# Second mixture: four weight buffers used for two groups, and the recurrence's tables begun a group later at four steps a group

## The chip, the cores and the metric

The kernel runs on one core of a Trainium2 chip. The metric is the device time of one execution in microseconds (us). A core has five engines with a queue of instructions each: PE (TensorE, matmuls), DVE (VectorE), ACT (ScalarE), POOL (GpSimd) and SP (SyncE, which here does little but issue loads). Sixteen DMA engines move data between the chip's DRAM and the core's SBUF; here transfers are issued by SP and, for a few small things, by ACT. An engine takes its instructions in order, and an instruction waits on semaphores for what it needs.

## What is computed

The program is two blocks in a row. The first has two layers, each a mixer (attention) and a mixture of experts; the second is a dilated attention and a recurrence (a diagonal state space model). The mixture, cut to what matters here:

```python
def hier_moe(xt, wg, bg, we, be, w1, w3, w2):
    ...                       # two experts of 32 and a weight for each token
    def expert_block(args):
        xb, e = args
        hb = jax.nn.silu(xb @ w1[e]) * (xb @ w3[e])
        return hb @ w2[e]
    ...                       # weighted, and added to the tokens
```

An expert has w1 and w3 of 1024 x 512 and w2 of 512 x 1024, 6 MB in float32. The recurrence of the last block:

```python
    A = lax.complex(a_re.astype(f), a_im.astype(f))
    dt = jnp.exp(log_dt.astype(f))[:, None]
    a_bar = jnp.exp(A * dt)
    Bm = lax.complex(b_re.astype(f), b_im.astype(f))
    b_bar = ((a_bar - 1.0) / A)[..., None] * Bm
    ...
    _, states = lax.associative_scan(combine, (a_elems, bu), axis=1)
    y = jnp.einsum('bsgp,gcp->bsgc', states, Cm).real
```

Powers of a_bar, b_bar and products of both with C depend on parameters alone. The kernel makes tables of them long before the recurrence, beside the second mixture.

## The kernel before

**The mixture's groups.** The second layer's mixture (`moe(1)`) has 256 tokens and works through all 32 experts in ten groups, p0 to p9 (`groups`, L1330): p0 and p1 take two experts each with 64 token slots, p2 to p5 three experts with 64, 32 and 32 slots, p6 to p9 four with 32. Each group's weights are loads of 1 MB, six for each expert: 12 loads in p0 and in p1, 18 in p2 to p5, 24 in p6 to p9, 192 in all. `weights` (L1134) issues them on SP in the order h0 w1, h0 w3, h1 w1, h1 w3 (h is the half of the 1024 rows), then w2. "Load 13 of p5" counts them from 0 within a group; loads 1 to 24 without a group are those of p0 and p1 counted from 1.

**One group on PE.** `hidden` (L1258) has four blocks of matmuls L1264, called h0m0, h0m1, h1m0, h1m1 (m 0 is w1, m 1 is w3); each uses one load of each expert. Between their matmuls `scatter` puts the result of the group before back to its tokens (L1314, L1315 on PE, products yt L1317 on DVE, sums L1321 on POOL); with two blocks of tokens that is four pieces, all in h0m0 and h0m1. Then the next group's tokens are gathered (L1225, L1251), and `result` (L1290) multiplies by w2 (L1296); ACT and DVE take it out of PSUM as yh and yl (L1303, L1304). The one-hot matrix of the next group is made on DVE ahead of hidden's scatter.

**The weight buffers.** `slot` (L136) gives a load its buffer. From this mixture's start the ring has 11 (7 named wt, 4 named wu), used in turn, so that a load waits for PE to be done with the load eleven ring loads before it. Beside it `early_slots` opens a pool of four buffers of the same size (named we) on the other side of SBUF; it lives until `rest` (L1076) closes it. Before, only loads 9 to 12 of p0, its h1 parts of w1 and w3, come there. The ring's loads are freed by PE's hidden and result. SP issues in program order, so a load that waits holds up all behind it.

**The tables.** `rest()` is called once, in p1: it closes the early pool, opens another at its place (`xl`), loads the final gain (fg) and starts the generator `side = self.ssm_side(...)` (L1797). Each `next(side)` emits one step of the tables in place, on whatever engines it needs. `hidden` calls it after h0m0 and h0m1 (condition `h == 0`), and `groups` calls it once more behind the result: three steps a group from p1 on. The 24 steps, as far as they matter:

- step 1: five small loads on ACT's queue (L1816, L1820) and four loads of 256 KB on SP through the ring, called raw 0 to 3 (the matrices of B and C)
- step 2: two transposes (L1844) and an exponential on DVE
- step 3: PE transposes raw 0 and 1 (L1836); step 5 those of raw 2 and 3
- steps 4 and 6: small DVE work; step 7 is empty; step 8: powers of a_bar on DVE (L1923 to L1969)
- step 9: b_bar (L1989 to L2001); step 10: Bg of the first half (L2012, L2014, with POOL)
- step 11: 16 transposes of Bg (L2021), copied to cx, then a write of 1 MB to DRAM on ACT's queue, Sd<-cx (L2024)
- step 12: Wd on DVE (L2031, L2032); step 13: KC (matmuls L2037, DVE L2040, L2042), then a write of 128 KB, Sm<-KC (L2044)
- steps 14 to 17: the same as 10 to 13 for the second half; steps 18 to 24: small writes of CP, E and U (L2053), powers on DVE and POOL, at the end two writes of 1 MB

A step of a group stands in the program where it is called, and that sets the order on every engine: the whole stage is under `manual_schedule`, which keeps the written order.

**The completion counters.** Transfers issued by SP and ACT take eight counters in turn (DMAHW0 to 7 in the rows below). A transfer waits for the one before it on its counter, whichever queue issued that. So a weight load can wait for a table write that ACT has not yet issued.

Of the kernel before, what the change touches and what calls it, by code (L numbers as in the profile page):

```python
# [27 lines left out]
NRING = 7  # L28
NMORE = 4
NBMAX = 16  # L30
FIRST = 1
EARLY = (1, 4)
SOON = 3
AFF = "aaaa"
# [83 lines left out]
class Model:  # L118
# [17 lines left out]
    def slot(self):  # L136

        self.load += 1
        if self.early is not None and self.load > self.early[1]:
            pool, _, n = self.early  # L140
            if self.load - self.early[1] == n:
                self.early = None
            return pool.tile([P, 2048], F32, name="we", tag="w")
        if self.cycle:
            self.turn += 1
            return self.cycle[(self.turn - 1) % len(self.cycle)].tile([P, 2048], F32, name="wu", tag="w")
        if self.apart:
            return self.ring2.tile([P, 2048], F32, name="wu", tag="w")
        self.turn += 1
        n = NRING + self.nmore  # L150
        if self.ring2 is not None and (self.turn * self.nmore % n < self.nmore if self.mixed else
                                       (self.turn - 1) % n >= NRING):
            return self.ring2.tile([P, 2048], F32, name="wu", tag="w")
        return self.ring.tile([P, 2048], F32, name="wt", tag="w")
# [4 lines left out]
        self.turn = self.load = 0  # L159
        ctx.callback(self.fewer_slots)  # L160

    def early_slots(self, ctx, name, n):

        self.early = ctx.enter_context(self.tc.tile_pool(name=name, bufs=n, side="right")), 12 - n, n

    def fewer_slots(self):
        self.ring2 = self.cycle = None
# [855 lines left out]
    def moe(self, l):  # L1023
        nc, A, tc, m = self.nc, self.A, self.tc, self.m
        nb, nv, ctx, c2, pool, sb, pr = m.nb, m.nb // 2, m.ctx, m.c2, m.pool, m.sb, m.pr
# [42 lines left out]
        side, G2 = iter(()), None if l == 0 else m.G2  # L1068
# [27 lines left out]
        def slots(ts):  # L1096

            at = [32 * sum(ts[:j]) for j in range(len(ts) + 1)]
            rs = [slice(a, b) for a, b in zip(at, at[1:])]
            w = 64 if ts == PAIR else 32  # L1100
            return rs, [(j, slice(a, a + w)) for j, r in enumerate(rs) for a in range(r.start, r.stop, w)]
# [116 lines left out]
        def gather(OH, rv, ts, pxs=None):  # L1218

            xg = xe.tile([P, D], F32, name="xg")  # L1220
            for n in range(2):
                px = pxs[n] if pxs else m.pp.tile([P, 512], F32, name=f"px{n}")
                for i in range(nb if pxs is None else 0):
                    for src in (hh, hl):
                        nc.tensor.matmul(px, lhsT=OH[:, i, :], rhs=src[:, i, 4 * n:4 * n + 4, :],  # L1225
                                         start=(i == 0 and src is hh), stop=(i == nb - 1 and src is hl))
                if n == 0:
                    nc.scalar.activation(xg[:, 0:512], px, AF.Copy)
                else:
                    nc.vector.tensor_copy(xg[:, 512:], px)  # L1230
            pid = psum.tile([P, 512], F32, name="tr", bufs=2)
            for i in range(nb):
                nc.tensor.matmul(pid[:, 0:4 * len(ts)], lhsT=OH[:, i, :], rhs=rv[:, i, :], start=(i == 0),
                                 stop=(i == nb - 1))
            sv = xe.tile([P, 4], F32, name="sv", bufs=2)
            for j, r in enumerate(slots(ts)[0]):
                nc.vector.tensor_copy(sv[r], pid[r, 4 * j:4 * j + 4])
            tk = xe.tile([P, nb], F32, name="tk")
            nc.vector.tensor_tensor(tk, sv[:, 0:1].to_broadcast([P, nb]), self.cc("blk")[:, 0:nb], op=ALU.subtract)
            nc.vector.tensor_add(sv[:, 1:2], sv[:, 1:2], sv[:, 2:3])  # L1240
            OT = xe.tile([P, nb, P], F32R, name="OT", bufs=2)
            nc.vector.tensor_tensor(OT, self.cc("iota")[:, None, :].to_broadcast([P, nb, P]),
                                    tk[:, :, None].to_broadcast([P, nb, P]), op=ALU.is_equal)
            return xg, (OT, sv, ts)

        def turn(xg):
            xT = xe.tile([P, NK, P], F32, name="xT")
            for n in range(2):
                pt = psum.tile([P, 4, P], F32, name="tr", bufs=2)
                for q in range(4):  # L1250
                    nc.tensor.transpose(pt[:, q, :], xg[:, (4 * n + q) * P:(4 * n + q + 1) * P], self.ident)  # L1251
                if n == 0:
                    nc.scalar.activation(xT[:, 0:4], pt, AF.Copy)
                else:
                    nc.vector.tensor_copy(xT[:, 4:8], pt)
            return xT

        def hidden(ws, xT, between=iter(()), turn=True, ts=PAIR):  # L1258
            ph = [psum.tile([P, 512], F32, name=f"ph{m}") for m in range(2)]
            for h in range(2):  # L1260
                for m in range(2):
                    for k in range(4 * h, 4 * h + 4):
                        for j, r in slots(ts)[1]:
                            nc.tensor.matmul(ph[m][r, :], lhsT=xT[:, k, r], rhs=ws[m, j, h][:, k % 4, :],  # L1264
                                             start=(k == 0), stop=(k == NK - 1))
                        if k % 2 == 1:
                            next(between, None)
                    if h == 0 and turn:
                        next(side, None)
            for _ in between:  # L1270
                pass

            sg = xe.tile([P, 512], F32, name="sg", tag="sg")
            sv = sg.rearrange("p (h k c) -> p h k c", h=2, k=2)
            pv = [v.rearrange("p (h c k) -> p h k c", h=2, k=2) for v in ph]
            nc.scalar.activation(sv, pv[0], AF.Sigmoid)  # L1276
            nc.vector.tensor_mul(sv, sv, pv[0])
            nc.vector.tensor_mul(sv, sv, pv[1])
            return sg
# [50 lines left out]
        def groups(todo):  # L1330

            with tc.manual_schedule():
                es = (0, 1)
                xg, at = gather(m.OH, RV[:, :, 0:2, :].rearrange("p t e c -> p t (e c)"), PAIR, m.px)
                xT = turn(xg)
                done = None
                for p, g in enumerate(todo):
                    ts = tuple(t for _, t in g)
                    more = p + 1 < len(todo)
                    if more and p >= len(fixed):  # L1340

                        nx = experts(order, [e for e, _ in todo[p + 1]])
                    ws = weights(es, 0 if p else EARLY[l])
                    if l == 1 and not more:
                        for _ in side:
                            pass
                        nc.gpsimd.tensor_copy(self.cx[:, 0], m.fg)
                        nc.gpsimd.tensor_tensor(m.fg, m.fg, m.fg, op=ALU.mult)
                    if more:
                        if p < len(fixed):  # L1350
                            nx = [e for e, _ in todo[p + 1]]
                            nx = experts(order, nx) if p + 1 == len(fixed) else nx
                        es = nx
                        oh = onehot(es, None, tuple(t for _, t in todo[p + 1]))
                    if p == 0:
                        blocks()
                    if p == 1:
                        rest()
                    sg = hidden(ws, xT, scatter(done) if done else iter(()), p >= FIRST, ts)
                    at0 = at  # L1360
                    if more:
                        xg, at = gather(*oh)
                    else:
                        nc.scalar.activation(self.stats[:, 5:6], self.cc("tokid")[:, 0:1], AF.Sqrt)
                    hT = turn_h(sg)
                    if more:
                        xT = turn(xg)
                    done = result(ws, hT, at0)
                    if p >= FIRST:
                        next(side, None)  # L1370
                for _ in scatter(done, True):
                    pass
                self.next_stats(l, xe)
# [49 lines left out]
    def phase_b(self):  # L1423
        nc, A, tc = self.nc, self.A, self.tc
        ctx = ExitStack()
        po_ = ctx.enter_context(tc.tile_pool(name="pbo", bufs=1, side="right"))
        c2 = ExitStack()
        ctx, cr = c2, ctx
        pool = ctx.enter_context(tc.tile_pool(name="pb", bufs=1))
# [138 lines left out]
        self.moe_open(1, OT, cr)  # L1568
        self.out_proj(wo, OT, 1, wp)
        cw.close()  # L1570
        self.early_slots(self.m.c4, "early1", EARLY[1])


    def bias_table(self, pool, wk, psum):
# [776 lines left out]
```

## Time and profile before

| what | value |
| --- | --- |
| median of 3 runs | 2048.04 us (2046.0 to 2048.42) |
| the profiled execution | 2048.95 us |
| its span (first to last instruction) | 2047.2 us |
| mean granted TensorE clock | 0.945 of full speed |
| busy: PE, DVE, ACT, POOL | 1772.8, 1090.9, 595.6, 593.3 us |
| bytes moved by DMA | 581.71 MB, 284 GB/s over the span |

The second mixture lies from about 1020 to 1540 us. The page's DMA line, a digit of tenths for each fortieth of the span, shows it as the stretch of 9s after a 5 and two 7s and 8s in the middle. PE reads as busy for 87% of the span; a busy PE there is also one whose matmuls stand behind a load. Two views matter more: the same busy times by stretch with the share of the DMA engines (a share of 1 means that all 16 were busy throughout; it can read a per cent or so more), and the timeline of an engine, whose brackets tell how long it sat idle before an instruction and what ended the wait. On SP a row is an issue; the time between two issues is the wait of the later one.

### The profile page before, as it was taken

Reading aid. Unit: us, or ns where it says so; the run is one execution under the profiler, and the core shown is the slowest. Engines: PE = TensorE matmul, PEld = TensorE weight load, DVE = VectorE, ACT = ScalarE, POOL = GpSimd, SP = SyncE. Lnnn points to the kernel's source line nnn. Section 1 sums busy time; section 2 is a strip of 40 time slices with the busy share of each in tenths; the row PEclk is TensorE's granted clock in tenths of the full one; section 3 lists DMA queues with packets and bytes.
Section 4 is the critical chain, followed back from the end, with each engine's and each line's share of the span. In section 5 each row is a group of like instructions: output and inputs, shape, how many; then the busy total and the mean of one; then the engine's idle time right before and its main releaser. Section 6 shows DMA issues by size and latency. Waiting matters only on the chain. (4 is left out here: it accounts for less than half of the span.)

```text
span 2047.2 us, 29948 instructions
## 1 busy us (share of the span) xinstructions
PE 1772.8 (87%) x11305; PEld 1056.6 (52%) x11305; DVE 1090.9 (53%) x2192; ACT 595.6 (29%) x1049; POOL 593.3 (29%) x467
## 2 busy tenths in 40 slices
PE   6999979999999976999978878777668999998978
PEld 3745744333333315777633222212217899986867
DVE  3565573333333326554565655553216777676884
ACT  3244321100100104434321100000005555554654
POOL 1210231323223224322211133232014443351552
PEclk9999979999999987999988989989898999998989
DMA  9375649999999975854579999999996545455041
GB/s 354 150 287 192 226 161 377 421 420 420 421 419 420 420 300 158 264 183 151 222 290 378 424 394 425 423 424 426 425 405 212 175 136 164 137 170 196 2 150 47
DMA packets 177860, 581.71 MB, mean 284 GB/s; under 512 B 28600, under 2 KB 97676, under 8 KB 127472
## 3 DMA queue, kind: packets, MB, share of 16 engines
q1 hardware_dynamic: 160208, 561.49, 70.4%
q10 hardware_dynamic: 15440, 11.10, 1.7%
q0 software_dynamic: 2064, 7.15, 1.1%
q8 instruction: 91, 1.49, 0.3%
q14 instruction: 57, 0.47, 0.1%
HBM read 572.38 MB, written 12.37 MB: 286 GB/s over the span
## 5 line engine op out<-in xcount | busy, mean ns | idle before, releaser
L1264 PE MATMUL ph<-wu,xT 128*32 128x512 f32 (+1 forms) x1744 | 364.6, 614 | 23.9 <-DMA wu<-in_moe_w_dram 23.8
L1321 POOL TENSOR_TENSOR x<-x,yt 128x512 f32<-128x512 f32 x88 | 113.6, 1296 | 569.4 <-DVE yt L1317 569.4
L209 DVE TENSOR_TENSOR wl<-wt,wh 128x1024 fp32r<-128x1024 f32 x121 | 190.1, 1588 | 63.5 <-ACT wh L206 49.9
L1264 PE MATMUL ph<-wt,xT 128*32 128x512 f32 (+1 forms) x712 | 183.1, 639 | 41.3 <-DMA wt<-in_moe_w_dram 41.3
L1317 DVE TENSOR_TENSOR yt<-px,G 128x512 f32<-128x512 f32 x144 | 98.4, 689 | 201.3 <-PE px L1315 196.9
L491 PE MATMUL mm<-hh,wh 128*128 128x256 f32 (+1 forms) x704 | 193.6, 301 | 4.2 <-ACT hh L462 2.1
L1296 PE MATMUL py<-wu,hTe 128*32 128x512 f32 (+1 forms) x888 | 181.9, 624 | 10.0 <-DMA wu<-in_moe_w_dram 5.3
L491 PE MATMUL mm<-hh,wl 128*128 128x256 f32 (+1 forms) x704 | 190.3, 297 | 0.0
L491 PE MATMUL mm<-hl,wh 128*128 128x256 f32 (+1 forms) x704 | 189.6, 295 | 0.0
L206 ACT ACTIVATE wh<-wt 128x1024 fp32r<-128x1024 f32 x162 | 163.8, 1050 | 73.3 <-PE mm L491 28.7
L1264 PEld LDWEIGHTS ph<-wu,xT 128*32 128x32 f32 (+1 forms) x1744 | 80.4, 116 | 179.3 <-issue 126.3
L209 POOL TENSOR_TENSOR wl<-wt,wh 128x1024 fp32r<-128x1024 f32 x41 | 107.9, 2631 | 131.2 <-ACT wh L206 106.0
L1304 DVE SCALAR_TENSOR_TENSOR yl<-py,sv,yh 128x512 fp32r<-128x512 f32 x46 | 34.5, 751 | 199.5 <-ACT yh L1303 199.5
L491 PEld LDWEIGHTS mm<-hh,wh 128*128 128x128 f32 x704 | 131.9, 195 | 12.1 <-ACT hh L462 3.7
L491 PEld LDWEIGHTS mm<-hh,wl 128*128 128x128 f32 x704 | 132.3, 195 | 3.5 <-issue 0.8
L491 PEld LDWEIGHTS mm<-hl,wh 128*128 128x128 f32 x704 | 131.7, 193 | 3.3 <-DVE hl L463 0.3
L1276 ACT ACTIVATE sg<-ph 128x512 f32<-128x512 f32 x23 | 13.7, 597 | 383.2 <-PE ph L1264 338.6
L1264 PEld LDWEIGHTS ph<-wt,xT 128*32 128x32 f32 (+1 forms) x712 | 38.3, 116 | 124.8 <-DMA wt<-in_moe_w_dram 71.3
L1296 PE MATMUL py<-wt,hTe 128*32 128x512 f32 (+1 forms) x360 | 89.5, 665 | 11.1 <-DMA wt<-in_moe_w_dram 11.1
L1296 PEld LDWEIGHTS py<-wu,hTe 128*32 128x32 f32 (+1 forms) x888 | 46.1, 120 | 91.9 <-issue 71.3
L1303 ACT ACTIVATE yh<-py,sv 128x512 fp32r<-128x512 f32 x46 | 31.6, 687 | 204.5 <-PE py L1296 204.5
L1314 PEld LDWEIGHTS px<-yh,OT 128*128 128x128 f32 x144 | 27.3, 190 | 123.6 <-issue 103.5
(614 smaller groups left out, 3478.3 us busy)
## 6 DMA issues: line engine op xcount, KB each, us to landing
wu<-in_moe_w_dram SPq DMA_DIRECT2D x259, 1024.0 KB
wt<-in_moe_w_dram SPq DMA_DIRECT2D x120, 1024.0 KB
wt<-in_ada_w_dram SPq DMA_DIRECT2D x40, 1024.0 KB
wt<-in_attn_w_in_dram SPq DMA_DIRECT2D x80, 512.0 KB
wt<-in_odd_w_in_dram SPq DMA_DIRECT2D x12, 1024.0 KB
wu<-in_ada_w_dram SPq DMA_DIRECT2D x8, 1024.0 KB
wt<-in_ssm_w_in_dram SPq DMA_DIRECT2D x6, 1024.0 KB
wt<-in_even_w_in_dram SPq DMA_DIRECT2D x5, 1024.0 KB
```

Of the source, the lines that this page charges most:

```text
L206: nc.scalar.activation(hi, v, AF.Copy)
L209: (nc.gpsimd if self.part % 4 == 3 else nc.vector).tensor_tensor(lo, v, hi.bitcast(F32), op=ALU.subtract)
L491: r = self.nc.tensor.matmul(out, lhsT=lhs[k][a], rhs=rhs[k][b], start=(start and i == 0), stop=(stop and i == 3 * n - 1))
L1264: nc.tensor.matmul(ph[m][r, :], lhsT=xT[:, k, r], rhs=ws[m, j, h][:, k % 4, :], start=(k == 0), stop=(k == NK - 1))
L1276: nc.scalar.activation(sv, pv[0], AF.Sigmoid)
L1296: nc.tensor.matmul(py[n][r, :], lhsT=hT[:, k, r], rhs=ws[2, j, k // 2][:, k % 2, n * 512:(n + 1) * 512], start=(k == 0), stop=(k == 3))
L1303: nc.scalar.activation(yh[:, c], py[n], AF.Copy, scale=sv[:, 1:2])
L1304: nc.vector.scalar_tensor_tensor(yl[:, c], py[n], sv[:, 1:2], yh[:, c].bitcast(F32), op0=ALU.mult, op1=ALU.subtract)
L1314: nc.tensor.matmul(pc, lhsT=OT[:, i, :], rhs=yh[:, c], start=True, stop=False)
L1317: nc.vector.tensor_mul(t, pc, G2[:, i // 2, c])
L1321: nc.gpsimd.tensor_tensor(xs[i][:, c], xs[i][:, c], t, op=ALU.add)
```

## The change

Three things change.

1. `early_slots` takes a list of loads, and the second mixture's is 9 to 12 and 20 to 23. So the last hidden load of p1 and three of its w2 loads use the four early buffers again, and the ring is four loads shorter of use at that point.
2. `rest()` is called in p2 instead of p1 (`p == l + 1`; for the first mixture, l = 0, it stays p1), and the steps begin in p2 (`FIRST` is 2). The final gain, the small loads and the raws stand behind the weight loads of p2 in the program.
3. `hidden` calls a step after h1m0 too (`h + m < 2`): four steps a group. Steps 1 to 4 are in p2, 5 to 8 in p3, 9 to 12 in p4, 13 to 16 in p5, 17 to 20 in p6, 21 to 24 in p7; before, three each in p1 to p8. The fourth of each group stands behind the result, the others behind h0m0, h0m1 and h1m0.

```diff
-FIRST = 1
+FIRST = 2
...
-        if self.early is not None and self.load > self.early[1]:
-            pool, _, n = self.early
-            if self.load - self.early[1] == n:
+        if self.early is not None and self.load in self.early[1]:
+            pool, at = self.early
+            if self.load == at[-1]:
                 self.early = None
             return pool.tile([P, 2048], F32, name="we", tag="w")
...
-    def early_slots(self, ctx, name, n):
+    def early_slots(self, ctx, name, n, again=()):
 
-        self.early = ctx.enter_context(self.tc.tile_pool(name=name, bufs=n, side="right")), 12 - n, n
+        self.early = ctx.enter_context(self.tc.tile_pool(name=name, bufs=n, side="right")), [*range(13 - n, 13), *again]
...
-                    if h == 0 and turn:
+                    if h + m < 2 and turn:
                         next(side, None)
...
-                    if p == 1:
+                    if p == l + 1:
                         rest()
...
-        self.early_slots(self.m.c4, "early1", EARLY[1])
+        self.early_slots(self.m.c4, "early1", EARLY[1], (20, 21, 22, 23))
```

On SP, the last five weight loads of p1 before (a number behind a name is the buffer's own; "waits" lists the counters and engines):

```order
L175 DMA wt_8483<-in_moe_w3_dram 128x2048 [waits DMAHW5_49,PE_49]
L175 DMA wu_8485<-in_moe_w2_dram 128x2048 [waits DMAHW2_49,PE_49]
L175 DMA wt_8487<-in_moe_w2_dram 128x2048 [waits DMAHW4_49,PE_49]
L175 DMA wt_8489<-in_moe_w2_dram 128x2048 [waits DMAHW5_49,PE_49]
L175 DMA wu_8491<-in_moe_w2_dram 128x2048 [waits DMAHW6_49,PE_49]
```

and now, the same five loads:

```order
L175 DMA we_8483<-in_moe_w3_dram 128x2048 [waits DMAHW5_49,PE_49]
L175 DMA we_8485<-in_moe_w2_dram 128x2048 [waits DMAHW6_49,PE_49]
L175 DMA we_8487<-in_moe_w2_dram 128x2048 [waits DMAHW7_49,PE_49]
L175 DMA we_8489<-in_moe_w2_dram 128x2048 [waits DMAHW0_49,PE_49]
L175 DMA wt_8491<-in_moe_w2_dram 128x2048 [waits DMAHW1_49,PE_49]
```

Four of them take early buffers (we); the fifth and the 18 loads of p2 move up four places in the ring.

On PE, step 3 before: behind the last matmuls of the result of p1 (L1296) and ahead of h0m0 of p2 (wu_8756 is its first load; wt_8556 and wu_8558 are raw 0 and 1):

```order
L1296 MATMUL py1_8677<-wu_8491,hTe_8660 64x512
L1836 MATMUL tr_8700<-C_66,wt_8556 64x64 [waits DMAHW0_49,Activation_49]
L1836 MATMUL tr_8700<-C_66,wt_8556 64x64 x7
L1836 MATMUL tr_8711<-C_66,wt_8556 64x64 [waits DVE_49]
L1836 MATMUL tr_8711<-C_66,wt_8556 64x64 x7
L1264 MATMUL ph0_8804<-wu_8756,xT_8663 32x512 [waits DMAHW4_49]
```

and now, inside the hidden layer of p2 (wt_8675 and wu_8677 are loads 7 and 8 of p2, wt_8679 load 9; wt_8756 and wu_8758 are raw 0 and 1):

```order
L1264 MATMUL ph0_8714<-wt_8675,xT_8612 32x512
L1264 MATMUL ph0_8714<-wu_8677,xT_8612 32x512
L1836 MATMUL tr_8834<-C_66,wt_8756 64x64 [waits DMAHW2_49]
L1836 MATMUL tr_8834<-C_66,wt_8756 64x64 x7
L1836 MATMUL tr_8845<-C_66,wt_8756 64x64 [waits DVE_49]
L1836 MATMUL tr_8845<-C_66,wt_8756 64x64 x7
L1836 MATMUL tr_8856<-C_66,wu_8758 64x64 [waits DMAHW3_49,DVE_49]
L1836 MATMUL tr_8856<-C_66,wu_8758 64x64 x7
L1264 MATMUL ph1_8715<-wt_8679,xT_8612 32x512 [waits DMAHW0_49]
```

The transposes of step 3 moved from behind a result to between h1m0 and h1m1, and the four raws now stand on SP behind all 18 loads of p2.

On PE, step 11 in the hidden layer of p4 before (wu_9430 is load 5 of p4, of h0m1; wt_9432 is load 6, of h1m0):

```order
L1264 MATMUL ph1_9469<-wu_9430,xT_9329 32x512
L1314 MATMUL px1_9538<-yh_9376,OT_8991 128x512 [waits DVE_49]
L1315 MATMUL px1_9538<-yl_9377,OT_8991 128x512
L2021 MATMUL tr_9544<-C_66,Bg_9498 128x128 [waits DVE_49,PE_49]
L2021 MATMUL tr_9544<-C_66,Bg_9498 128x128 x3
```

and now (wt_9410 is load 8, of h1m0; wu_9412 is load 9, of h1m1):

```order
L1264 MATMUL ph0_9442<-wt_9410,xT_9272 32x512
L2021 MATMUL tr_9560<-C_66,Bg_9526 128x128 [waits DVE_49,PE_49]
L2021 MATMUL tr_9560<-C_66,Bg_9526 128x128 x3
L2021 MATMUL tr_9566<-C_66,Bg_9526 128x128 [waits PE_49]
L2021 MATMUL tr_9566<-C_66,Bg_9526 128x128 x3
L2021 MATMUL tr_9572<-C_66,Bg_9526 128x128 [waits Activation_49]
L2021 MATMUL tr_9572<-C_66,Bg_9526 128x128 x3
L2021 MATMUL tr_9578<-C_66,Bg_9526 128x128 [waits DVE_49]
L2021 MATMUL tr_9578<-C_66,Bg_9526 128x128 x3
L1264 MATMUL ph1_9443<-wu_9412,xT_9272 32x512 [waits DMAHW1_49]
```

The step moved behind h1m0, and steps 9 and 10 stand on DVE between the result of p3 and it, with step 8 ahead of both. The write that follows takes a counter from the eight, as do those of steps 13, 15 and 17. The weight load that takes the same counter next was load 16 of p4, load 14 of p5, load 9 of p6 and load 19 of p6 for the four writes before; now it is load 1 of p5, load 13 of p5, load 1 of p6 and load 12 of p6.

## Rows read from the trace of the kernel before

**Rows 1.** Busy time by stretch: us, engines, clock, DMA share, GB/s.

```profile
1058.00:1068.00 10.00, 8.71 (x47) 4.41 (x47) 2.86 (x9) 1.47 (x3) 0.00 (x0) 1.00 0.17 45
...
1084.00:1092.00 8.00, 7.34 (x38) 3.73 (x34) 6.13 (x26) 1.20 (x2) 0.00 (x0) 1.00 1.03 235
...
1096.00:1100.00 4.00, 4.00 (x22) 1.29 (x18) 0.33 (x1) 0.69 (x1) 0.00 (x0) 1.00 0.74 258
1100.00:1220.00 120.00, 92.82 (x656) 33.67 (x656) 72.88 (x212) 13.75 (x24) 29.68 (x23) 0.91 1.01 425
1220.00:1226.00 6.00, 4.75 (x34) 2.81 (x26) 2.81 (x9) 0.82 (x2) 0.00 (x0) 1.00 0.55 195
1226.00:1520.00 294.00, 220.36 (x1162) 62.71 (x1162) 122.64 (x241) 19.35 (x34) 62.69 (x51) 0.91 1.01 424
```

**Rows 2.** Timeline of SP, p0 and p1: start, us, instruction.

```profile
1051.05 15.61 SPq L175 DMA_DIRECT2D wt<-in_moe_w_dram  x2
```

**Rows 3.** Waits of the load queue from 1200 to 1232: total, times, longest.

```profile
SPq L175 <- DMA Sd<-cx: 19.3, 1, 19.3
```

**Rows 4.** Timeline of PE: start, us, instruction; here p0's hidden layer ends.

```profile
1057.40 0.50 PE L1225 MATMUL px<-OTh,OH 128*128 128x512 f32 x1
```

**Rows 5.** Timeline of SP, p4 to p6: the issues that ended long waits.

```profile
1224.58 0.33 SPq L175 DMA_DIRECT2D wu<-in_moe_w_dram  x1
...
1250.56 11.51 SPq L175 DMA_DIRECT2D wt<-in_moe_w_dram  x2
...
1295.80 0.91 SPq L175 DMA_DIRECT2D wt<-in_moe_w_dram  x2
...
1322.80 0.34 SPq L175 DMA_DIRECT2D wu<-in_moe_w_dram  x1
```

**Rows 6.** Timeline of PE, the result of p4 (its wait and its end).

```profile
1231.94 0.63 PE L1296 MATMUL py<-wt,hTe 128*32 128x512 f32 x3 [0.65 <-DMA wt<-in_moe_w_dram]
...
1234.97 0.59 PE L1296 MATMUL py<-wt,hTe 128*32 128x512 f32 x1
```

**Rows 7.** Timeline of PE, step 3 and the hidden layer of p3.

```profile
1100.49 1.12 PE L1836 MATMUL tr<-C,wt 64*64 64x64 f32 x16
...
1145.39 0.63 PE L1264 MATMUL ph<-wt,xT 128*32 128x512 f32 x3 [1.26 <-DMA wt<-in_moe_w_dram]
```

**Rows 8.** Timeline of PE, the hidden layer of p4.

```profile
1189.89 0.89 PE L1264 MATMUL ph<-wt,xT 128*32 128x512 f32 x1 [1.42 <-DMA wt<-in_moe_w_dram]
...
1210.88 3.55 PE L2021 MATMUL tr<-C,Bg 128*128 128x128 f32 x16 [8.36 <-DVE Bg L2014]
1214.36 0.63 PE L1264 MATMUL ph<-wt,xT 128*32 128x512 f32 x3
...
1221.37 0.50 PE L1225 MATMUL px<-OTh,OH 128*128 128x512 f32 x1
```

**Rows 9.** Timeline of DVE: steps 8, 9 and 10 (first rows, and the rows behind).

```profile
1158.63 0.11 DVE L1923 MEMSET Epow<- 128x64 f32 x1
...
1171.80 0.69 DVE L1277 TENSOR_TENSOR sg<-sg,ph 128x512 f32<-128x512 f32 x1
...
1187.56 0.68 DVE L1989 TENSOR_TENSOR x<-b,F 128x512 f32<-128x512 f32 x1
...
1210.65 1.28 DVE L1317 TENSOR_TENSOR yt<-px,G 128x512 f32<-128x512 f32 x2
```

**Rows 10.** Timeline of ACT: table writes issued.

```profile
1215.24 0.36 ACTq L2024 DMA_DIRECT2D Sd<-cx  x1
1254.73 0.33 ACTq L2044 DMA_DIRECT2D Sm<-KC  x1
1285.38 0.33 ACTq L2024 DMA_DIRECT2D Sd<-cx  x1
```

**Rows 11.** Timeline of PE, the hidden layers of p5 and p6.

```profile
1239.59 0.63 PE L1264 MATMUL ph<-wt,xT 128*32 128x512 f32 x3 [1.45 <-DMA wt<-in_moe_w_dram]
...
1320.16 0.62 PE L1264 MATMUL ph<-wt,xT 128*32 128x512 f32 x2 [1.48 <-DMA wt<-in_moe_w_dram]
```

## The prediction

> **What bounds the kernel now.** I read the second mixture in stretches first [rows 1]: from 1100 to 1220 and from 1226 to 1520 us the DMA share is 1.01 at 424 to 425 GB/s, so a weight load of 1,048,576 bytes takes 2.47 us, and PE waits for it. In that regime every microsecond in which the DMA engines idle is a microsecond of the kernel. Then the holes [rows 1]: 1058 to 1068 (share 0.17, so 8.3 us idle), 1096 to 1100 (0.74, 1.0 us idle) and 1220 to 1226 (0.55, 2.7 us idle). Last, who makes them. Before 1068 the load queue stands 15.61 us at a weight load of p1 [rows 2]: all eleven ring buffers are full, and the next one comes free only inside the result of p0. Before 1226 it stands 19.3 us on a table write, Sd<-cx [rows 3]. So the stage is worth 192 loads of 2.47 us plus the holes, and each edit is priced by what it does to a hole.
>
> **Part 1, the four early buffers again.** Loads 20 to 23 go to the four "we" buffers, which PE frees with h1m0 and h1m1 of p0, ahead of the gather at 1057.40 [rows 4], not to ring buffers freed inside the result, at 1066 and later. Four loads are 9.9 us of transfers, and the hole has 8.3 us. Starting costs something: the load released into the empty queues at 1224.58 [rows 5] was followed by a second one that let PE go on at 1231.94 [rows 6], so it landed about 1229.5, 4.9 us after its issue, 2.4 more than its own transfer. The first two "we" buffers come free about 3.5 us before 1057.40, so most of that start lies ahead of the hole. I count 7.5 us, plus the 1 us at 1096: the lead is **8.5 us** (5 to 10).
>
> **Part 2, the first steps of the tables, one group later.** With rest() and step 1 move 0.5 MB of final gain, four raw loads of 0.25 MB and five small loads on ACT's queue. They stood ahead of p2's loads; the stretch 1084 to 1092 shows their price, a full share at 235 GB/s [rows 1], some 7.5 us for 1.57 MB. The bytes stay; the place moves, and there I expect the loss. The raws take ring buffers behind all 18 loads of p2, so raw 0 needs the buffer of load 7 of p2 and raw 1 that of load 8, both freed when PE ends h1m0. But the transposes L1836 that read them (step 3) now stand on PE right behind h1m0 and ahead of h1m1. Before, they stood behind the result of p1 and ran at 1100.49 without a wait [rows 7].
>
> So p2 goes like this. The 3.6 us of step 3 leave p1, so hidden(2) begins about 1099. Two blocks with their scatter at 5 us each, L1844, and one block of 3.5 us (half of 1214.36 to 1221.37 [rows 8]) put the end of h1m0 at about 1114. Buffers limit the loads: load 10 gets one at about 1099, from the end of p1's result, 11 to 13 after h0m0, about 1103.5; so the DMA idles about 1095.5 to 1100 and 1102.7 to 1105. Loads 11 to 17 then take 17.3 us, to 1122.5; fg and raws 0 and 1 two thirds of 7.5 us, to about 1127. PE stands from 1114 to 1127. Then 3.6 us of transposes and 3.5 of h1m1, to 1134. Raws 2 and 3 and load 0 of p3 need buffers of h1m1, so the DMA is empty from 1127 to about 1135.4 (8.5 us), and again some 3.5 us until p2's result frees the next. That is 12 us idle against a lead of 8.5: load 2 of p3, which PE got at 1145.39 [rows 7], lands about 1149. **Parts 1 and 2 together: +4 us** (-4 if the raws come 8 us sooner, +7 if the restarts cost the 2.4 us of rows 5 and 6 more than I count).
>
> **Part 3, four steps a group: p4.** Let Z be the landing of load 2 of p4, 1189.9 [rows 8]. On DVE step 8 takes 13.1 us, 1158.63 to 1171.80, and stood inside hidden(3); it now follows the result of p3. The next pieces (step 9, the one-hot, two scatter products, step 10) took 23.1 us, 1187.56 to 1210.65 [rows 9]. In a row they end at Z - 2.3 + 13.1 + 23.1 = Z + 33.9, and with two more products the transposes L2021 start at Z + 35; before it was Z + 21, after 8.36 us of waiting [rows 8]. From L2021 to the issue of the write Sd<-cx are 4.4 us [rows 8, 10]: Z + 39.4. Behind it PE has h1m1, 5.4 us of gather and 7 of result, to Z + 54.4.
>
> Queued behind that write is the load queue: loads and ACT's transfers take eight completion counters in turn, and each waits for the last one on its counter. Before, the write held load 16 of p4, released at Z + 34.7 [rows 5], while load 15 had landed at Z + 13 x 2.47 = Z + 32.2. After, it holds load 1 of p5, and load 0 lands at Z + 39.6. A write into drained queues taken at 4.9 us, as the load above, frees it at Z + 44.3; load 1 lands at Z + 49.2, against Z + 44.6 unheld (the write's own 2.5 us counted): 4.6 us lost, 2.4 before. **+2 us** (-1 to +6, since among loads the write took 9.3 us [rows 5, 10]).
>
> The Trainium skill, page DMA: Bandwidth & Descriptors, section Issuing engines are not separate DMA queues, has transfers started by ScalarE and SyncE interleave on the same 16 engines. By it the 9.3 us are a write's price among loads, and in drained queues the first write is nearer +2 than +6; no row shows such a write.
>
> **Part 3 in p5 and p6.** The next three writes held loads too, but with slack. I move each slack by the loads in between and by the shift of the write against the loads.
> First KC: issued 1254.73 [rows 10], 19.3 us after the result of p4 ended (1235.4 [rows 6]), it held load 14 of p5 until 1262.1 [rows 5]. Load 2 landed at 1239.6 [rows 11], load 13 so at 1266.8: slack 4.7. After, it holds load 13 (-2.5), and the result of p4 ends 2.6 us after load 2 lands (Z + 51.8), not 4.2 before (-6.8). Of the -4.6 a faster landing gives back 3; a restart costs 2.4: 4 us lost.
> Second Sd: it held load 9 of p6 until 1295.80 [rows 5]; load 15 landed at 1320.16 [rows 11], load 8 so at 1302.8: slack 7.0. After, it holds load 1 (-19.8), but is issued 13 us sooner behind KC, since its transposes move into hidden(5), and the loads are 4 us later and its landing faster: 1 us lost. **Together +5** (0 to +9).
> Second KC: it held load 19 of p6 until 1322.80 [rows 5]; load 18 landed at 1327.6: slack 4.8. After, it holds load 12 (-17.3), with the write 4 us sooner against the loads and 3 us faster. **+5** (0 to +8). CP, E and U follow and hold loads 15 to 17 of p6: 0, covered by the hold before them, else +1.
> From p7 on steps go and none come; the tables are ready a group sooner and nothing at the end waits for them: 0.
>
> **Sum.** 4 + 2 + 5 + 5 = +16 us on the profiled run's 2048.95 us (its span is 2047.2). The median of the runs is 0.9 us lower, so **2064 us**.
>
> **Rivals.**
> (1) Faster. The raws overtake the weight loads queued ahead of them, PE doesn't stand at step 3, and the writes stay covered. Then the lead of 8.5 us is kept: **2040 us**. It decides at raw 1 landing by the end of h1m0, 1114 in place of 1127. For it: 0.25 MB is small beside what is queued. Against: it is issued only when h1m0 ends. The Trainium skill, page Trainium Kernel Development and Optimization, section Best Practices, asks to double-buffer so that DMA and compute overlap; by that alone the four slots are a plain gain, and this is its time.
> (2) About the same. PE stands at step 3, but the holds of p5 and p6 are covered, as all three were from 1226 to 1520 (share 1.01 [rows 1] with 11.51 us of waiting [rows 5]). Then +6, or 0 where step 3 stalls less: **2048 to 2054 us**.
> (3) Worse. A write into drained queues takes its 9.3 us all the same; the three terms of part 3 each lose 3 to 4 us more: **2075 us**.
> (4) The change doesn't do what it says, and loads 20 to 23 still wait. The queues lie empty where they would start [rows 1], so nothing is left to wait for but PE: no chance of its own.
>
> **How the numbers follow.** Forecast 0.55, rival 1 0.17, rival 2 0.20, rival 3 0.08. A measurement here can tell about 0.2%, 4 us, from no change. Faster: rival 1, 0.17. Same, 2044 to 2052: three quarters of rival 2, 0.15. Slower: the rest, 0.68. The terms' bounds let the forecast lie between 2053 and 2072; a range that leaves out 2 in 10 begins above rival 1, at 2043, and ends at 2073.
>
> **What would show it.** DMA share near 1 from 1058 to 1068 (part 1). PE idle some 13 us at L1836 behind h1m0 of p2, ended by a DMA, and empty queues for 8 us after it (part 2). PE waiting some 15 us at L2021 in p4, and shares under 1 where the writes of p4, p5 and p6 hold the load queue (part 3). I am wrong if L1836 finds its raws in place, or if the share stays at 1.01 from p4 on.

## The result: 21 us slower, and the profile after

The changed kernel takes 2069.1 us (median of 5 runs, 2067.23 to 2074.51) against 2048.04 us. The ratio is 1.011, with a 95% interval of 1.0096 to 1.0124, so 20 to 25 us slower. The forecast was 2064, slower.

One thing first about comparing profiled runs. Up to 1040 us both kernels execute the same code, yet the changed one's profiled run is 7.6 us ahead at the end of p0 (the second yl of p0 at 1062.98, against 1070.54 before); over the twelve profiles of this study that point lies between 1063.0 and 1070.5. So I compare a stage length inside one trace: from the second yl of p0 (L1304 on DVE) to the second yl of p9. Before, its two ends are

```profile
1070.54 0.75 DVE L1304 SCALAR_TENSOR_TENSOR yl<-py,sv,yh 128x512 fp32r<-128x512 f32 x1 [0.99 <-ACT yh L1303]
...
1530.98 0.75 DVE L1304 SCALAR_TENSOR_TENSOR yl<-py,sv,yh 128x512 fp32r<-128x512 f32 x1 [0.91 <-ACT yh L1303]
```

and now

```profile
1062.98 0.75 DVE L1304 SCALAR_TENSOR_TENSOR yl<-py,sv,yh 128x512 fp32r<-128x512 f32 x1 [0.99 <-ACT yh L1303]
...
1547.09 0.75 DVE L1304 SCALAR_TENSOR_TENSOR yl<-py,sv,yh 128x512 fp32r<-128x512 f32 x1 [0.91 <-ACT yh L1303]
```

The stage was 460.4 us before and is **484.1 us** now. The 23.7 us between them are the change; what follows the stage is 516.2 us before and 518.3 now.

The busy times of the changed kernel by stretch, in order of time; columns as in [rows 1], the last two being DMA share and GB/s:

```profile
1058.00:1068.00 10.00, 10.00 (x46) 3.21 (x44) 4.05 (x13) 1.37 (x2) 1.17 (x1) 1.00 0.99 397
...
1087.00:1099.00 12.00, 12.00 (x76) 3.44 (x72) 4.06 (x13) 1.37 (x2) 2.56 (x2) 1.00 0.57 187
...
1119.00:1135.00 16.00, 13.62 (x90) 7.71 (x94) 6.24 (x14) 4.32 (x8) 0.00 (x0) 0.71 0.30 91
1135.00:1143.00 8.00, 7.84 (x70) 2.14 (x70) 1.64 (x3) 1.38 (x2) 0.00 (x0) 1.00 0.80 298
1143.00:1223.00 80.00, 52.94 (x352) 17.41 (x352) 54.43 (x176) 5.70 (x10) 20.72 (x16) 0.86 1.01 425
1223.00:1239.00 16.00, 11.76 (x70) 7.00 (x70) 7.37 (x15) 3.26 (x6) 4.38 (x4) 0.76 0.62 246
...
1263.00:1271.00 8.00, 8.00 (x57) 2.20 (x60) 4.33 (x6) 0.00 (x0) 2.39 (x2) 0.89 0.66 244
...
1283.00:1291.00 8.00, 7.89 (x51) 3.78 (x50) 2.77 (x5) 1.79 (x3) 0.19 (x1) 0.86 0.51 209
...
1315.00:1323.00 8.00, 8.00 (x38) 1.80 (x36) 5.93 (x8) 0.00 (x0) 1.57 (x2) 0.73 0.52 216
...
1335.00:1339.00 4.00, 2.79 (x16) 0.81 (x20) 3.73 (x7) 0.00 (x0) 2.46 (x2) 0.68 0.63 179
```

Multiply each length by one minus its share. The hole that the four buffers were put at is gone (1058 to 1068: 0.99, before 0.17; 1050 to 1058, the same place less the 7.6 us, reads 1.01). New holes stand at 1087 (5.2 us), 1119 (11.2), 1135 (1.6), 1223 (6.1), 1263 (2.7), 1283 (3.9), 1315 (3.8) and 1335 (1.5): 36.0 us. The three holes of [rows 1] were 12.0 us; the first of them ends just ahead of the stage's first mark, and counts because the loads that it delayed land inside the stage. The difference, 24.0 us, is close to the stage's 23.7. Between the holes the share is 0.99 to 1.01.

Who makes the new holes: PE's timeline at the two places where it stands longest,

```profile
1119.37 1.92 PE L1836 MATMUL tr<-C,wt 64*64 64x64 f32 x16 [13.83 <-DMA wt<-in_ssm_b_re_dram]
...
1225.78 3.84 PE L2021 MATMUL tr<-C,Bg 128*128 128x128 f32 x16 [18.09 <-DVE Bg L2014]
```

and the load queue's waits from 1100 to 1400 (in total, times, longest), to be read against [rows 3] and [rows 5]:

```profile
SPq L175 <- DMA Sd<-cx: 37.1, 2, 22.1
...
SPq L175 <- DMA Sm<-KC: 31.2, 2, 16.6
...
SPq L175 <- DMA Sm<-CP: 11.9, 1, 11.9
SPq L175 <- DMA wt<-in_ssm_b_re_dram: 11.7, 1, 11.7
```

Step 3 waits 13.83 us for raw 0, in the middle of p2's hidden layer; step 11 waits 18.09 us for DVE, where it waited 8.36 before [rows 8]; and the two Sd writes hold a load 22.1 and 15.0 us, KC 16.6 and 14.6, with holes behind all four.

### The profile page after: what moved, and what is told of

The parts are those of the page before. It is cut to its first block, busy times and chain, and to the rows that moved or that the text cites. A ratio compares the mean times of both kernels' runs of the same rounds, so it can differ in the third digit from the quotient of the medians.

```text
span 2065.4 us, 29958 instructions
## 1 busy us (share of the span) xinstructions
PE 1771.2 (86%) x11305; PEld 1059.2 (51%) x11305; DVE 1083.2 (52%) x2192; ACT 596.2 (29%) x1049; POOL 591.8 (29%) x467
## 3 DMA queue, kind: packets, MB, share of 16 engines
q0 software_dynamic: 2064, 7.15, 1.1%
## 5 line engine op out<-in xcount | busy, mean ns | idle before, releaser
L1264 PE MATMUL ph<-wt,xT 128*32 128x512 f32 (+1 forms) x688 | 177.7, 657 | 28.0 <-DMA wt<-in_moe_w_dram 28.0
L206 ACT ACTIVATE wh<-wt 128x1024 fp32r<-128x1024 f32 x162 | 163.9, 1050 | 71.8 <-PE mm L491 28.6
L1296 PE MATMUL py<-wu,hTe 128*32 128x512 f32 (+1 forms) x848 | 170.6, 624 | 6.7 <-DMA wu<-in_moe_w_dram 3.3
L1304 DVE SCALAR_TENSOR_TENSOR yl<-py,sv,yh 128x512 fp32r<-128x512 f32 x46 | 34.5, 751 | 195.3 <-ACT yh L1303 195.3
L1296 PE MATMUL py<-wt,hTe 128*32 128x512 f32 (+1 forms) x376 | 86.7, 665 | 12.8 <-DMA wt<-in_moe_w_dram 12.3
L1321 POOL TENSOR_TENSOR cx<-cx,yt 128x512 f32<-128x512 f32 x50 | 63.9, 1278 | 76.7 <-DVE yt L1317 76.7
```

The costliest lines, as they stand in the source:

```text
L206: nc.scalar.activation(hi, v, AF.Copy)
L1296: nc.tensor.matmul(py[n][r, :], lhsT=hT[:, k, r], rhs=ws[2, j, k // 2][:, k % 2, n * 512:(n + 1) * 512], start=(k == 0), stop=(k == 3))
L1304: nc.vector.scalar_tensor_tensor(yl[:, c], py[n], sv[:, 1:2], yh[:, c].bitcast(F32), op0=ALU.mult, op1=ALU.subtract)
L1321: nc.gpsimd.tensor_tensor(xs[i][:, c], xs[i][:, c], t, op=ALU.add)
```

## Experiments

All times are medians; ratios are to the kernel before, run on the same chip. "Stage" is the length defined above, from the one profiled run of each kernel.

**Three steps a group, all else as changed.** This undoes part 3 alone.

```diff
-                    if h + m < 2 and turn:
+                    if h == 0 and turn:
```

> The changed kernel with three steps a group again (condition h == 0); the four early buffers and the start of the tables in p2 stay, so step 3 stands behind the result of p2 and each table write one group later than before. My theory (the loss is step 3 inside the hidden layer of p2, worth 11 to 13 us of empty DMA queues there, and the writes of p4 to p6 holding the load queue, 18 us): both go, PE finds raw 0 and 1 in place at L1836, and the DMA idle of the stage falls from 42 us in the changed kernel to about 14 to 18: 2044 to 2049 us. Rival (the loss comes from moving fg and the raws behind p2's loads, or from the four buffers' place, whatever the step count): little changes, above 2060 us. Third case: a table write in p9 comes too late and the end of the stage waits for it, 2050 us or more with a hole at the end of p9.

Measured: 2040.17 us, ratio 0.9969 (0.9954 to 0.9984). It is not only quicker than the changed kernel but than the one before; stage 456.2 us. The stretches of its trace, columns as above, with PE's waits for raw 0 and for Bg:

```profile
1058.00:1068.00 10.00, 10.00 (x48) 3.52 (x49) 2.19 (x3) 1.65 (x3) 0.00 (x0) 1.00 0.99 396
...
1090.00:1102.00 12.00, 12.00 (x77) 3.51 (x74) 4.06 (x13) 1.38 (x2) 2.41 (x2) 1.00 0.62 203
1102.00:1200.00 98.00, 78.59 (x566) 27.29 (x565) 48.46 (x166) 11.99 (x21) 12.80 (x11) 0.97 1.01 408
...
1250.00:1264.00 14.00, 12.37 (x101) 5.55 (x104) 5.03 (x13) 2.38 (x5) 2.25 (x3) 1.00 0.76 304
1264.00:1520.00 256.00, 187.40 (x952) 51.08 (x948) 112.01 (x210) 15.27 (x26) 57.67 (x47) 0.91 1.01 421
```

```profile
PE tr L2021 <- DVE Bg L2014: 8.4, 1, 8.4
...
PE tr L1836 <- DMA wt<-in_ssm_b_re_dram: 0.3, 1, 0.3
```

Two holes are left after 1058: 4.6 us in p1, where the ring is full, and 3.4 us in p5, behind the first Sd. Both long stands of PE have gone back: 13.83 to 0.3 us, 18.09 to 8.4. So the whole loss hangs on the fourth step, the stall at step 3 included; the move to p2 and the four buffers together are a gain. The rival, by which the moved loads themselves cost, falls. No write came too late in p9.

**The empty step moved ahead of step 3.** Step 3 then stands behind the result of p2, and from step 8 on everything stands where the changed kernel has it.

```diff
         yield
+        yield
         turned(0)
 ...
-        yield
         yield
         E = p.tile([P, 5, 2, 64], F32, name="Epow")
```

> The changed kernel with the empty step (7) moved in front of step 3: the transposes of raw 0 and 1 stand behind the result of p2, and from step 8 on every step stands where the changed kernel has it. My theory: the 13.83 us wait of PE at L1836 goes and with it 11.1 + 1.7 us of empty DMA queues between 1119 and 1143; what happens from p4 on stays: about 2057 us (2053 to 2060). Rival (the stall at step 3 is paid for by loads that ran ahead, so taking it away moves the same idle time to the next full ring): 2064 us or more. If PE still waits for a raw behind the result of p2, the raws and not the place of the step are late.

Measured: 2059.21 us, ratio 1.0068 (1.0044 to 1.0093); stage 470.9 us, 13.2 less than the changed kernel's. The transposes find their raw:

```profile
1126.41 1.09 PE L1836 MATMUL tr<-C,wt 64*64 64x64 f32 x16 [0.35 <-DMA wt<-in_ssm_b_re_dram]
```

and from p4 on the holes are still there, here the four of p4 to p6:

```profile
1218.00:1230.00 12.00, 10.37 (x67) 6.34 (x67) 4.91 (x13) 2.88 (x6) 3.19 (x3) 0.87 0.49 185
...
1258.00:1262.00 4.00, 4.00 (x38) 1.11 (x30) 1.54 (x3) 0.00 (x0) 2.43 (x2) 1.00 0.30 74
...
1278.00:1286.00 8.00, 6.37 (x50) 3.56 (x42) 3.65 (x11) 1.47 (x3) 0.00 (x0) 1.00 0.63 231
...
1310.00:1318.00 8.00, 8.00 (x65) 2.21 (x58) 2.87 (x7) 0.00 (x0) 3.96 (x4) 1.00 0.61 215
```

6.1, 2.8, 3.0 and 3.1 us. The holes in p2 are worth about what they measured: 11.2 + 1.6 us of holes, 13.2 us of stage, some 9 us by the two ratios. The loads that now come earlier do not cover the holes behind.

**All table writes from POOL's queue, otherwise as changed.** In this program POOL's transfers take other completion counters than the loads, so no weight load can wait for one; the waits below bear it out.

```diff
-            nc.scalar.dma_start(self.Sd[hf], stage)
+            nc.gpsimd.dma_start(self.Sd[hf], stage)
 ...
```

(likewise at L2044, L2053 and L2103)

> The changed kernel with all table writes (Sd, KC, CP, E, U, and the last two of 1 MB) issued from POOL's queue instead of ACT's; these take other completion counters than the weight loads, so no load can be held by one. Steps and places are unchanged. My theory (the holes of p4, p5 and p6, together 18.2 us, are loads held by a counter): SP no longer waits for Sd or Sm, these holes fall to 2 us or less, PE still waits some 18 us at L2021 in p4: about 2052 us (2049 to 2056). Rival (the holes are PE's wait at L2021 and L2037, which keeps the ring's buffers full): the holes stay, 2064 us or more, with SP waiting for PE in place of DMA.

Measured: 2062.46 us, ratio 1.008 (1.0058 to 1.0101); stage 474.4 us, 9.7 less than the changed kernel's, where I expected the time to fall by 17. The waits of the load queue from 1200 to 1360 and the holes that stay:

```profile
SPq L175 <- PE ph L1264: 82.4, 11, 19.4
SPq L175 <- PE py L1296: 28.9, 8, 9.2
```

```profile
1234.00:1254.00 20.00, 18.54 (x143) 7.74 (x141) 7.03 (x16) 3.93 (x7) 2.69 (x3) 0.93 0.82 315
...
1270.00:1278.00 8.00, 8.00 (x64) 2.27 (x60) 3.40 (x5) 0.00 (x0) 3.85 (x4) 0.95 0.71 266
...
1290.00:1306.00 16.00, 14.38 (x115) 5.99 (x118) 4.94 (x13) 2.56 (x5) 2.66 (x3) 0.96 0.80 307
```

No load waits for a table write any more; the queue now waits for PE instead, and holes of 3.6, 2.3 and 3.2 us remain, 9.1 of the changed kernel's 18.0 in p4 to p6. So a held counter makes half of these holes. The other half is PE itself: it still stands 18.1 us at L2021, the ring's eleven buffers stay full, and the DMA engines run out of places. The load queue shows it behind step 11 of p4, where load 1 of p5 now goes at once and load 2 waits 19.4 us for PE's h1m1 behind the stand:

```profile
1218.07 0.33 SPq L175 DMA_DIRECT2D wt<-in_moe_w_dram  x1
1239.85 0.33 SPq L175 DMA_DIRECT2D wu<-in_moe_w_dram  x1
```

One load of 2.5 us is what the write held there: the hole is 3.6 us in place of 6.1. Theory and rival each had a half.

**No second use of the early buffers, otherwise as changed.**

```diff
-        self.early_slots(self.m.c4, "early1", EARLY[1], (20, 21, 22, 23))
+        self.early_slots(self.m.c4, "early1", EARLY[1])
```

> The changed kernel without the second use of the four early buffers (loads 20 to 23 go to the ring as before); all steps as in the changed kernel. It measures part 1 alone. By my prediction the buffers give a lead of 8.5 us that nothing takes back before p2: about 2077 us. By the trace of the changed kernel the ring runs full again in p1 (DMA idle 5.2 us between 1087 and 1099, where the kernel before had 0.8), so the buffers are worth only some 4 us: about 2073 us. If they were worth nothing here: 2069 us.

Measured: 2074.09 us, ratio 1.0149 (1.0117 to 1.0182); by the ratios that is 8 us above the changed kernel, but its stage is 486.0 us, only 1.9 more. The hole in p0 is back (1054 to 1066: 0.27, 8.8 us), that in p1 is gone, and at step 3 the hole is 10.9 us (11.2 and 1.6 with the buffers):

```profile
1054.00:1066.00 12.00, 10.71 (x56) 5.11 (x54) 3.34 (x9) 1.94 (x4) 0.00 (x0) 1.00 0.27 95
1066.00:1126.00 60.00, 43.27 (x238) 14.85 (x234) 19.40 (x62) 4.36 (x8) 10.15 (x8) 0.90 1.01 411
1126.00:1142.00 16.00, 11.82 (x76) 6.58 (x77) 4.26 (x7) 3.44 (x6) 0.00 (x0) 0.61 0.32 74
```

The holes agree with the stage: 19.7 us up to step 3 against 18.0 with the buffers. The times do not decide, since the two intervals meet (1.0117 here, 1.0124 there). So by its trace part 1 is worth some 2 us in the changed kernel, and by the times alone 8.5 us is not ruled out. The next pair measures it where no step stands in the way.

**Three steps a group, with and without the second use.** The same edit as above on the three-step kernel, and that kernel once more on the same chip.

> The three-step kernel (tables begun in p2, three steps a group) without the second use of the four early buffers. It measures the buffers where no step stands in the way. The three-step kernel had holes of 4.8 us (start) and 4.9 us (1090 to 1102) up to p2; the kernel before had 4.7, 8.8 and 0.8. Theory: the hole of 8 to 9 us after 1055 comes back and the one in p1 goes, so the buffers are worth some 4 us: 2043 to 2046 us. By the prediction's lead of 8.5 us: 2048 to 2050 us. If they are worth nothing: 2040 us.

> The three-step kernel with the four early buffers once more, on the same chip as the one without them, so that the two compare directly: 2040 us, 4 us below that one if the buffers are worth what the holes say, 8.5 us if they are worth the prediction's lead.

Measured: 2045.67 us without (0.9997, 0.9981 to 1.0012), 2041.90 with (0.9982, 0.9969 to 0.9994): 3.8 us apart, with intervals that overlap a little; the stages, 462.1 and 455.1 us, differ by 7.0, but they come from the slowest of the ten runs without (2051.23 us) and the fastest of the ten with (2039.42 us). The traces say why it is less than 8.5: without the second use 9.3 us of idle time lie between 1058 and 1074, with it 5.1 us between 1066 and 1102, 4.2 us fewer. So the buffers are worth some 4 us, 7 at most by these readings.

The run without them is also part 2 alone on the kernel before: three steps a group, the buffers used once, only the start moved to p2. Its ratio of 0.9997 says that the move by itself costs nothing that can be told here.

**Four steps a group alone, on the kernel before.** Tables begun in p1 and early buffers used once, as before; only the condition is changed.

```diff
-                    if h == 0 and turn:
+                    if h + m < 2 and turn:
```

> The kernel before with four steps a group alone (condition h + m < 2; tables begun in p1, early buffers used once). It measures part 3 alone. Theory: step 3 now stands behind h1m0 of p1, where its raws are issued at 1080 to 1085, before or about when h1m0 ends, so PE waits 4 to 8 us there in a stretch where the DMA has work; steps 8 to 11 follow each other from the result of p2 into hidden(3), so PE waits some 18 us at L2021, and three or four writes hold loads: 10 to 18 us more of holes, 2058 to 2066 us. Rival (four steps a group cost only because the start was moved to p2): 2046 to 2052 us.

Measured: 2075.13 us, ratio 1.0122 (1.01 to 1.0144); stage 490.5 us. I expected 2058 to 2066: the direction and the mechanism hold, the size was too low by 9 us. The same two stands are there, one group earlier:

```profile
PE tr L2021 <- DVE Bg L2014: 25.3, 2, 17.7
...
PE tr L1836 <- DMA wt<-in_ssm_b_re_dram: 4.4, 1, 4.4
```

```profile
1086.00:1102.00 16.00, 13.89 (x70) 8.00 (x70) 6.23 (x14) 4.31 (x8) 0.00 (x0) 0.70 0.63 217
...
1186.00:1202.00 16.00, 11.09 (x66) 6.50 (x66) 8.38 (x17) 2.39 (x4) 5.38 (x4) 0.73 0.36 136
```

The hole behind step 11 is 10.2 us here, 6.1 in the changed kernel; how much of it is held and how much is PE's stand I did not separate. What it settles: the fourth step costs 25 us (20 to 29) by itself, without any move.

**Both edits on the changed kernel, and POOL's queue on two others.**

> The changed kernel with both edits: the empty step ahead of step 3, and all table writes from POOL's queue. Theory so far: two causes that add up, the stand at step 3 (13 us of the stage from yl of p0 to yl of p9, 484.1 to 470.9 us in the traces) and the held loads (10 us, 484.1 to 474.4); what is left are holes of some 8 us in p4 to p6 where PE stands at L2021 and L2037 with the ring full. So a stage of about 461 us, as before the change (460.4): 2046 to 2051 us. Rival (the two overlap: without the stand the loads run further ahead and cover the held ones, or the reverse): a stage of 466 us or more, above 2053 us.

> The kernel before with all table writes from POOL's queue. The one hole that a held load makes there (1220 to 1226, 2.7 to 3 us) goes: a stage of 457 to 458 us (460.4 before), 2044 to 2046 us. If PE's wait of 8.36 us at L2021 makes the hole, it stays: 2048 us.

> The changed kernel with three steps a group and all table writes from POOL's queue. The three-step kernel had 456.2 us of stage and one hole of 3.4 us at a held load in p5; without the hold about 453 us of stage and 2037 to 2040 us, the lowest of all. Rival (POOL's start of the writes, in order behind its own work, delays the scatter sums): the same as the three-step kernel or slower, 2040 us or more.

Measured: the first 2050.97 us, ratio 1.0018 (1.0006 to 1.0029), stage 465.0 us, where I expected 461. The two causes add up, nearly: 13.2 + 9.7 = 22.9 us apart, 19.1 together. PE's stands at L2021 and L2037 are still in it, and 4.6 us more of stage than before. The three-step kernel with POOL's writes, below, where PE waits 8.4 us at L2021 in place of 18.1, has 12.1 us less of stage (452.9): that much the fourth step still costs with both other causes gone, and since no load waits for a table write in either, it goes through PE. The kernel before with POOL's writes: 2043.43 us, 0.9981 (0.9967 to 0.9995); its one hole at a held load is gone, though its profiled stage came out at 460.4 us again, with 2.2 us lost in p1 and 2.1 in p9, where nothing was edited; the profiled run was the slowest of its ten (2050.6 us). The three-step kernel with POOL's writes: 2040.16 us, 0.9956 (0.9937 to 0.9976), stage 452.9 us. Behind p1's hole it has none to the end of the stage:

```profile
1090.00:1106.00 16.00, 16.00 (x102) 4.78 (x98) 4.80 (x15) 1.37 (x2) 3.84 (x3) 1.00 0.66 232
1106.00:1520.00 414.00, 314.59 (x1802) 97.01 (x1800) 197.33 (x471) 34.73 (x60) 93.17 (x80) 0.90 1.01 419
```

It and the plain three-step kernel beat both kernels of this case; the intervals of the two overlap, so which of them is quicker stays open.

## Why the prediction was right, step by step

**The frame held.** Loads of 2.47 us plus holes: 24.0 us more of holes, 23.7 us more of stage.

**Parts 1 and 2, +4 forecast, +8.7 measured in holes** (5.2 + 11.2 + 1.6 of new ones, less 8.3 + 1.0). The stall came as described: PE at L1836 for 13.83 us (forecast 13), released by raw 0, with the queues empty for 12.8 us after it (forecast 12). The term that was mis-sized is the lead. I let the buffers bring 8.5 us and set only the 12 us of p2 against it; but the idle time in p1 that I had myself written down (1095.5 to 1100 and 1102.7 to 1105, 6.8 us) comes off that lead first. It measured 5.2 us at 1087 to 1099. By the three-step pair the buffers are worth some 4 us. The hole was moved from p0 to p1 more than it was filled.

How much of the miss that explains depends on the mark. The prediction also had a clock, which ran through those 6.8 us and still put load 2 of p3 only 3.6 us later (1149 against 1145.39 [rows 7]), so its two countings do not agree with each other. In the changed kernel PE got that load at

```profile
1143.45 0.62 PE L1264 MATMUL ph<-wt,xT 128*32 128x512 f32 x1 [0.60 <-DMA wt<-in_moe_w_dram]
```

80.5 us after the second yl of p0, against 74.9 before: +5.6. Load 2 of p4, the prediction's Z, came +7.0 (at 1189.30, before at 1189.89 [rows 8]). So parts 1 and 2 cost 2 to 5 us more than forecast. A smaller slip: 1.57 MB at 235 GB/s are 6.7 us, not the 7.5 written for the final gain and the raws.

**p4, +2 forecast, +3.4 measured** (6.1 less 2.7). The chain on DVE brought L2021 to 36.5 us after Z (1225.78 less 1189.30), forecast 35. Its first row and the last of step 8:

```profile
1186.99 0.11 DVE L1923 MEMSET Epow<- 128x64 f32 x1
...
1197.06 0.35 DVE L1969 COPY U<-sv 64x32 f32<-64x32 f32 x3
```

The sum is near by luck in part: step 8 took 10.4 us here, not the 13.1 of [rows 9], and what follows it 28.4 us, not 24.2. PE's wait grew from 8.36 to 18.09 us, since steps 9 and 10 come behind step 8. Sd then held load 1 of p5, which SP issued 22.6 us after load 0:

```profile
1211.84 0.33 SPq L175 DMA_DIRECT2D wu<-in_moe_w_dram  x1
1234.45 0.33 SPq L175 DMA_DIRECT2D wt<-in_moe_w_dram  x1
```

The write was issued at 1230.42, so the load was released 4.0 us later, and behind the second Sd 5.2 us later (1284.83 to 1290.04): a write into drained queues is near the 4.9 us that I took, not the 9.3. But I priced the hole by the hold alone; with POOL's writes 3.6 of the 6.1 us remain, which are PE's stand.

**p5 and p6, +5 and +5 forecast, +6.6 and +5.3 measured** (2.7 + 3.9, 3.8 + 1.5). The slacks were used up as worked out: KC and Sd in p5 and KC in p6 each made a hole, and CP made one of 1.5 us where I had written 0, else +1. What was wrong is the reason in part: I put all of it to the held counter. The run with POOL's writes shows that the hold makes half of the 18.0 us of p4 to p6, and PE's stands at L2021 and L2037 with a full ring the rest. That the sum came near in spite of this is luck in part: the two lie on top of each other. In p4, counted from the start of L2021, the write let load 1 go after 8.7 us, and the buffer for load 2 came free after 7.9 (in the run with POOL's writes).

**The sum.** 16 us were forecast, 21 measured, 23.7 in the stage; 2 to 5 of the missing 7.7 lie in parts 1 and 2, the rest in p4 to p6. Rival 1 (2040 us) asked for both raws by the end of h1m0, and even raw 0 came 13.83 us after it. Rival 2 asked for covered holds, and none of the four was. Rival 3, a write of 9.3 us in drained queues, is out by the 4.0 and 5.2 us above, though the time lies about midway between the forecast and it.

Two rules were weighed. That transfers of ScalarE and SyncE interleave on the same engines (the Trainium skill, DMA: Bandwidth & Descriptors, section Issuing engines are not separate DMA queues) fits the write's 4.0 and 5.2 us against 9.3 among loads. The page also says that issuing from several engines saves only the time to issue; here the engine that issued made 9.7 us of stage, not through the engines but through the counter that a load shares with the write. To double-buffer (the Trainium skill, Trainium Kernel Development and Optimization, section Best Practices) was worth 3.8 us, by the three-step pair.

## What to carry to other kernels

In a stretch bound by its transfers, price an edit by the time in which the DMA engines idle, and follow a gained lead to the next place where the buffers are full before you count it. Spread side work by what the main stream waits for, not by finishing it early: these tables had groups to spare, and one step more a group put a transpose ahead of the data it reads and a chain of DVE work ahead of PE, 25 us for nothing gained. Look up which earlier transfer each load's counter waits for; a small write from another queue can hold a whole weight stream, and issuing it elsewhere was the cheapest edit of this study.

## What the runs showed of the hardware

PE did not come back from its stand at full speed. The granted clock from 1119 to 1128 in the changed kernel is 0.50, the lower of its two levels (1.2 GHz), after 13 us without a matmul; then 0.98:

```profile
1106.00:1119.00 13.00, 0.00 (x0) 0.00 (x0) 2.08 (x10) 0.00 (x0) 0.00 (x0) 0.57 1.01 395
1119.00:1124.00 5.00, 4.09 (x36) 3.52 (x40) 1.81 (x3) 1.99 (x4) 0.00 (x0) 0.50 0.25 61
1124.00:1128.00 4.00, 4.00 (x24) 0.84 (x20) 1.61 (x3) 0.86 (x2) 0.00 (x0) 0.50 0.00 0
1128.00:1135.00 7.00, 5.54 (x42) 3.35 (x38) 2.81 (x9) 1.47 (x3) 0.00 (x0) 0.98 0.51 164
```

The block h1m1 behind the stall so took 5.8 us (1123.68 to 1129.48) for the 3.5 I had counted, and for most of that time the queues were empty. The spread between executions that have the same code up to 1040 us, 7.5 us at the second yl of p0, was also more than I had expected; it is why a few microseconds here are read from a stage and not from a whole span.
